# An alignment directive in VectorE's instruction stream, in a log-sum-exp kernel

## Chip, cores and metric

The kernel runs on one core of one Trainium2 chip. The metric is the device time of one execution in microseconds (us), as the median of several. A profiled execution of its own shows where the time goes; its span runs from the first to the last of the program's own instructions.

The engines, as the profile names them: PE is TensorE's matmul and PEld its weight load, DVE is VectorE, ACT is ScalarE, POOL is GpSimd, SP is SyncE. A letter q behind a name means the engine's sequencer: a branch, a semaphore, a register load or the issue of a DMA, during which the engine itself does not compute. Each engine has its own stream of instructions.

## Reference

```python
def reference(x):                       # x: 32 x 512 x 1024, float32
    max_x = np.max(x, axis=-1, keepdims=True)
    return (max_x.squeeze(-1) + np.log(np.sum(np.exp(x - max_x), axis=-1))).astype(np.float32)
```

For each of the 16384 rows of 1024 numbers, one number comes out: the logarithm of the sum of the exponentials.

## The kernel before

The kernel does not subtract the maximum. It computes log(sum(exp(x))) directly, checks that all sums are in a safe range, and only if they are not takes a slow path that does subtract it. The data drawn here are normal, so the slow path is never entered; it stands in the program and is jumped over.

Rows are spread over 128 partitions, 128 rows for each. The input (67 MB) is brought in by 18 loads, all issued by SyncE, whose sizes and treatment the table LOADS lists: three of 16 rows for each partition, then ever smaller ones, the last ones of 0.75 to 1.7 rows. They go into a ring of 48 rows in SBUF. A load waits for those who still use its place in the ring (line 128).

For each load ScalarE takes the exponential in place (line 209). The sum of a row is then made in one of three ways, by the letters of the table: R is a reduction on VectorE (line 220); G lets GpSimd add the right half of each row to the left (line 215), and VectorE reduces the left half later (line 146); T is one VectorE instruction for each row that adds the two halves and accumulates the sum as it goes (line 154, the helper `add_halves`). In the profile each T shows as two rows, a SCALAR_TENSOR_TENSOR and the DVE_READ_ACCUMULATOR behind it. The very last row is split: three quarters of it are summed by ScalarE itself in its exponential (line 204, letter b), the rest by VectorE (letter a).

The order of each engine's instructions is the order in which the Python loop over the loads (line 174) emits them; there is no scheduler. The waits are written by hand: each engine counts a semaphore up with every instruction, and others wait for a count. For the last loads VectorE's stream is: two halves-adding instructions each for the loads with T2, one each for the loads with T1, one for the last (T1+a) and one of 128 columns for the split row. Eight of them come before the sixteenth load (index 15), three after it.

At the end (lines 240 to 264) ScalarE takes the logarithm of the last sums (lines 245 and 247) and SyncE stores them (line 251). At the same time VectorE condenses the sums into a check (lines 161 and 165), TensorE adds the check over the partitions (lines 171, 172 and 255), and VectorE compares the result with a bound (line 259). ScalarE and VectorE both load that flag into a register (line 262) and branch (line 311 in the profile): past the slow path, which has ten instructions on VectorE (lines 288 to 305), or into it. Behind it each of the two counts up the semaphore `done` (lines 311 and 312). SyncE waits for both, clears the semaphores (line 315) and waits for the last store (line 317).

## Time and profile before

| | us |
|---|---|
| median of 3 executions | 162.78 |
| lowest and highest of them | 162.53, 162.91 |
| the profiled execution | 162.55 |
| its span | 161.2 |
| VectorE busy in the span | 119.1 |
| ScalarE busy in the span | 115.1 |
| GpSimd busy in the span | 32.4 |

The input moves at a mean of 417 GB/s over the span. The profiled execution's own time is 1.35 us longer than its span: what lies ahead of the program's first instruction and behind its last. Instructions of a sequencer are not counted as busy; they are found by their source line. In a timeline row the first number is the start and the second the length, both in us.

### The profile page before, as it was taken

Reading aid. Unit: us, or ns where it says so; the run is one execution under the profiler, and the core shown is the slowest. Engines: PE = TensorE matmul, PEld = TensorE weight load, DVE = VectorE, ACT = ScalarE, POOL = GpSimd, SP = SyncE. Lnnn points to the kernel's source line nnn. Section 1 sums busy time; section 2 is a strip of 40 time slices with the busy share of each in tenths; the row PEclk is TensorE's granted clock in tenths of the full one; section 3 lists DMA queues with packets and bytes.
Section 4 is the critical chain, followed back from the end, with each engine's and each line's share of the span. In section 5 each row is a group of like instructions: output and inputs, shape, how many; then the busy total and the mean of one; then the engine's idle time right before and its main releaser. Section 6 shows DMA issues by size and latency. Waiting matters only on the chain.

```text
span 161.2 us, 183 instructions
## 1 busy us (share of the span) xinstructions
PE 0.5 (0%) x10; PEld 0.3 (0%) x10; DVE 119.1 (74%) x48; ACT 115.1 (71%) x32; POOL 32.4 (20%) x15
## 2 busy tenths in 40 slices
PE   0000000000000000000000000000000000000000
PEld 0000000000000000000000000000000000000000
DVE  0000000019999499995999999999999999999995
ACT  3000059980799609994199928996997999799995
POOL 0000000000000000000008800007950806727600
DMA  7996996996996996997999989898998999999990
GB/s 276 504 520 276 504 520 276 504 520 293 488 520 293 488 520 293 488 520 325 429 469 469 469 376 424 377 483 385 454 454 384 419 439 411 409 429 414 424 407 12
DMA packets 2880, 67.18 MB, mean 417 GB/s; under 512 B 576, under 2 KB 576, under 8 KB 1344
## 3 DMA queue, kind: packets, MB, share of 16 engines
q1 hardware_dynamic: 2880, 67.18, 97.2%
HBM read 67.11 MB, written 0.07 MB: 417 GB/s over the span
## 4 chain that ended last, share of the span: by engine, by line
DVE 53%; DMA 30%; ACT 12%; POOL 4%; PE 0%; issue 0%
DVE sumexp L220 38%; DMA ring<-in_x_dram 30%; ACT ring L209 12%; DVE sumexp L146 10%; POOL ring L215 4%; DVE ring L154 4%; DVE clamped L161 1%; DVE total L165 0%; PE count L171 0%; DVE fine L259 0%; PE count L255 0%; PE count L172 0%
## 5 line engine op out<-in xcount | busy, mean ns | idle before, releaser
L209 ACT ACTIVATE ring<-ring 128x16384 f32<-128x16384 f32 (+22 forms) x26 | 112.4, 4371 | 42.7 <-DMA ring<-in_x_dram 42.6
L220 DVE TENSOR_REDUCE sumexp<-ring 128x16 f32<-128x16384 f32 (+6 forms) x10 | 96.1, 9639 | 40.0 <-ACT ring L209 40.0
L215 POOL TENSOR_TENSOR ring<-ring 128x1024 f32<-128x1024 f32 (+5 forms) x9 | 32.1, 3573 | 118.3 <-ACT ring L209 118.3
L146 DVE TENSOR_REDUCE sumexp<-ring 128x2 f32<-128x1024 f32 (+5 forms) x9 | 16.1, 1802 | 0.4 <-POOL ring L215 0.4
L154 DVE SCALAR_TENSOR_TENSOR ring<-ring 128x512 f32<-128x512 f32 (+1 forms) x11 | 6.5, 642 | 0.0
L118 ACT ACT_TABLE_LOAD x1 | 1.3, 1283 | 1.4 <-PEq L59 1.4
L161 DVE SCALAR_TENSOR_TENSOR clamped<-sumexp 128x114 f32<-128x114 f32 (+1 forms) x2 | 0.9, 472 | 0.1
L204 ACT ACTIVATE ring<-ring 128x768 f32<-128x768 f32 x1 | 0.8, 843 | 0.1
L171 PE MATMUL count<-far,bad 128*1 128x1 f32 x4 | 0.4, 163 | 159.1 <-DVE total L165 159.1
L154 DVE DVE_READ_ACCUMULATOR ring<-ring 128x1 f32 x11 | 0.8, 76 | 0.0
L171 PEld LDWEIGHTS count<-far,bad 128*1 128x1 f32 x4 | 0.2, 80 | 159.2 <-POOL ring L215 151.1
L259 DVE TENSOR_SCALAR fine<-count 1x1 int32<-1x1 f32 x1 | 0.1, 146 | 0.4 <-PE count L255 0.4
L165 DVE TENSOR_REDUCE total<-sumexp 128x1 f32<-128x114 f32 (+1 forms) x2 | 0.4, 210 | 0.0
L172 PE MATMUL count<-total,ones 128*1 128x1 f32 x4 | 0.4, 163 | 0.0
L245 ACT ACTIVATE res<-sumexp 128x15 f32<-128x15 f32 x1 | 0.2, 215 | 0.1
L119 POOL MEMSET ones<- 128x1 f32 x1 | 0.1, 98 | 1.0 <-POOLq L59 1.0
L195 ACT ACTIVATE res<-sumexp 128x112 f32<-128x112 f32 x1 | 0.3, 280 | 0.0
L247 ACT ACTIVATE res<-sumexp 128x1 f32<-128x1 f32 x1 | 0.3, 278 | 0.0
L172 PEld LDWEIGHTS count<-total,ones 128*1 128x1 f32 x4 | 0.2, 81 | 0.0
L255 PE MATMUL count<-sumexp,ones 128*1 128x1 f32 x2 | 0.2, 163 | 0.0
L204 ACT ACTIVATION_READ_ACCUMULATOR ring<-ring 128x1 f32 x1 | 0.2, 187 | 0.0
L161 DVE DVE_READ_ACCUMULATOR clamped<-sumexp 128x1 f32 x2 | 0.2, 79 | 0.0
(6 smaller groups left out, 0.6 us busy)
## 6 DMA issues: line engine op xcount, KB each, us to landing
ring<-in_x_dram SPq DMA_DIRECT2D x1, 7376.0 KB, 24.9
ring<-in_x_dram SPq DMA_DIRECT2D x1, 5936.0 KB, 19.6
ring<-in_x_dram SPq DMA_DIRECT2D x1, 4768.0 KB, 16.4
ring<-in_x_dram SPq DMA_DIRECT2D x1, 3520.0 KB, 15.2
ring<-in_x_dram SPq DMA_DIRECT2D x1, 2976.0 KB, 21.9
ring<-in_x_dram SPq DMA_DIRECT2D x1, 1792.0 KB, 27.6
ring<-in_x_dram SPq DMA_DIRECT2D x1, 1520.0 KB, 25.2
ring<-in_x_dram SPq DMA_DIRECT2D x1, 1360.0 KB, 19.5
```

The lines of the kernel that those rows point to most:

```text
L118: nc.scalar.preload_act_table_set("natural_log_exp_and_others")
L146: at = dve.did(nc.vector.reduce_sum(out=sumexp[:, c0 : c0 + s], in_=half, axis=AX.X))
L154: return dve.did(nc.vector.scalar_tensor_tensor(out=lo, in0=lo, scalar=1.0, in1=v[:, h : 2 * h], op0=ALU.mult, op1=ALU.add, accum_out=sume ...
L161: dve.did(nc.vector.scalar_tensor_tensor(out=clamped[:, c0:c1], in0=sumexp[:, c0:c1], scalar=LOW, in1=sumexp[:, c0:c1], op0=ALU.max, op1=A ...
L165: at = dve.did(nc.vector.reduce_sum(out=total[:, k : k + 1], in_=sumexp[:, c0:c1], axis=AX.X))
L171: pe.did(nc.tensor.matmul(count, lhsT=bad[:, k : k + 1], rhs=far, start=k == 0, stop=False))
L172: pe.did(nc.tensor.matmul(count, lhsT=ones, rhs=total[:, k : k + 1], start=False, stop=False))
L195: ln_early = act.did(nc.scalar.activation(out=res[:, 0:W], in_=sumexp[:, 0:W], func=AF.Ln))
L204: last = act.did(nc.scalar.activation(out=v, in_=v, func=AF.Exp, accum_out=sumexp[:, NC : NC + 1]))
L209: at = act.did(nc.scalar.activation(out=v, in_=v, func=AF.Exp))
L215: folded.append((c, p, s, pool.did(nc.gpsimd.tensor_tensor(out=rows[:, :, 0:H], in0=rows[:, :, 0:H], in1=rows[:, :, H:d], op=ALU.add,))))
L220: users.append((p, p + s * d, dve, dve.did(nc.vector.reduce_sum(out=sumexp[:, c : c + s], in_=rows, axis=AX.X))))
```

## The change

A constant names the sixteenth load (index 15), and in the loop, when that load's turn comes, a directive is put into VectorE's stream before its next instruction. It asks the loader to place what follows at a slot whose number is a multiple of 128, and to fill the slots in between with empty instructions. Only VectorE's stream has it. All instructions, waits and loads that were there stay in their order.

```diff
 B = 16
+
+ALIGNED = 15
...
         act.wait(landed[i], 16)
+        if i == ALIGNED:
+            nc.vector.addr_align(128)
         for k, part in enumerate(parts):
```

The next instruction on VectorE after the directive is the halves-adding instruction of that load (line 154, line 156 with the change), the ninth of eleven.

## The prediction

> **What bounds the kernel now.** I read the page first, then the chain of waits in its last microseconds, then VectorE's timeline there, and last the single source lines whose instructions are the sequencers' own and so count as busy nowhere. The page:

> ```profile
> span 161.2 us, 183 instructions
> PE 0.5 (0%) x10; PEld 0.3 (0%) x10; DVE 119.1 (74%) x48; ACT 115.1 (71%) x32; POOL 32.4 (20%) x15
> DVE 53%; DMA 30%; ACT 12%; POOL 4%; PE 0%; issue 0%
> ```

> No engine is full over the whole span; VectorE (DVE) holds more than half of the chain that ends last. The end of that chain, from the view of the chain of waits:

> ```profile
> 155.16 3.89 DVE ring L154 x14
> 159.05 0.02 issue
> 159.07 0.18 DVE clamped L161 x2
> 159.25 0.09 DVE total L165
> 159.34 0.04 issue
> 159.39 0.19 PE count L171 x2
> ...
> 159.71 0.15 DVE fine L259
> ```

> The reader should see two things. From 155.16 to 159.05 any delay of VectorE is a delay of the end. And the chain stops at 159.86 (159.71 + 0.15), while the span ends at 161.2: 1.34 us follow in which no engine is busy. The timeline and the single lines show what stands there:

> ```profile
> 159.50 0.34 SPq L251 DMA_DIRECT2D out_dram<-res  x1
> ...
> L262 ACTq TENSOR_LOAD <-fine x1: 463/463/463, 159.9 to 159.9; - x1
> L262 DVEq TENSOR_LOAD <-fine x1: 544/544/544, 159.9 to 159.9; - x1
> ...
> L311 ACTq COMPARE_BRANCH  x1: 45/45/45, 160.4 to 160.4; - x1
> L311 DVEq COMPARE_BRANCH  x1: 67/67/67, 160.5 to 160.5; - x1
> L311 ACTq EVENT_SEMAPHORE  x1: 17/17/17, 160.5 to 160.5; - x1
> ...
> L312 DVEq EVENT_SEMAPHORE  x1: 21/21/21, 161.0 to 161.0; - x1
> ...
> L315 SPq EVENT_SEMAPHORE_RANGE_CLEAR  x1: 71/71/71, 161.1 to 161.1; - x1
> ...
> L317 SPq EVENT_SEMAPHORE  x1: 17/17/17, 161.2 to 161.2; - x1
> ```

> Durations are in ns, starts in us. ScalarE (ACT) and VectorE both load the flag, branch over the slow path, and count up `done`. ScalarE's branch ends at about 160.4 + 0.045 and its count-up starts at 160.5: 0.1 us between. VectorE's load starts at 159.9 and takes 0.544, so its branch runs at about 160.47 to 160.54; its count-up starts only at 161.0 (160.95 to 161.05). That is 0.41 to 0.51 us for the same jump. SyncE waits for that count-up and then ends the kernel:

> ```profile
> SPq L315 <- DVEq L312: 1.2, 1, 1.2
> ```

> So the tail is set by VectorE's jump, 0.3 to 0.4 us longer than ScalarE's. The other thing the end waits for is the landing of the last store:

> ```profile
> out_dram<-res SPq DMA_DIRECT2D x1, 8.0 KB, 1.4
> ```

> Issued at 159.50, it lands at 160.85 to 160.95 (1.4 as printed), 0.25 to 0.35 before the end: hidden now, but not by much.

> **The change part by part.** One directive goes into VectorE's stream, between the eighth and the ninth of the halves-adding instructions (line 154). No wait, DMA, buffer or arithmetic is added, removed or moved. Two things follow: a filling ahead of the ninth, N slots with N from 0 to 127, and everything behind it lies elsewhere relative to the borders of the blocks in which code is fetched. The place, from VectorE's timeline:

> ```profile
> 154.48 0.67 DVE L146 TENSOR_REDUCE sumexp<-ring 128x1 f32<-128x512 f32 x1
> 155.08 0.67 DVE L154 SCALAR_TENSOR_TENSOR ring<-ring 128x512 f32<-128x512 f32 x1
> ...
> 156.91 0.68 DVE L154 SCALAR_TENSOR_TENSOR ring<-ring 128x512 f32<-128x512 f32 x1
> 157.52 0.07 DVE L154 DVE_READ_ACCUMULATOR ring<-ring 128x1 f32 x1
> 157.52 0.68 DVE L154 SCALAR_TENSOR_TENSOR ring<-ring 128x512 f32<-128x512 f32 x1
> ...
> 158.75 0.28 DVE L154 SCALAR_TENSOR_TENSOR ring<-ring 128x128 f32<-128x128 f32 x1
> 158.96 0.08 DVE L154 DVE_READ_ACCUMULATOR ring<-ring 128x1 f32 x1
> ```

> *Why a jump may be dear.* That code is fetched by DMA in pieces shows in the DMA view of the stretch 161 to 163 us, just after VectorE's jump:

> ```profile
> GB/s 0 0 0 0 0 0 0 0 0 0 0 0 164 0 0 0 0 0 0 0 0 0 0 0 0 0 0 0 0 0 0 0 0 0 0 0 0 0 0 0
> q14 instruction: 1, 0.01, 1.7%
> ```

> One packet of the kind "instruction", at 161.60 to 161.65: 164 GB/s over a slice of 0.05 us is 8.2 KB. The queue table of the page has none inside the span. So somewhere near the end one engine went over the border of a fetched piece and the next was sent for. My reading is that it was VectorE, that its border lies between the branch and its target, and that the extra 0.3 to 0.4 us is the price of going over it.

> [...]

> *The filling.* If the border is there, N can be counted. Behind the directive stand three pairs of line 154, a pair of line 161, lines 165 and 259, the load and the branch: twelve instructions. The slow path has ten more, then the count-up. So the border lies 12 to 22 slots behind the directive, and aligning pulls it forward by that many: N is 12 to 22. The price of an empty slot is not in the trace; the nearest rows:

> ```profile
> L59 DVEq DRAIN  x2: 10/10/10, 0.8 to 1.2; - x2
> L59 DVEq EVENT_SEMAPHORE  x2: 21/21/21, 1.1 to 1.4; - x2
> ...
> 0.23 0.10 POOL L355 MEMSET const-float32-0.0<- 128x1 f32 x1 [0.23 <-issue]
> ...
> 0.34 0.10 POOL L355 MEMSET const-uint8-127<- 128x1 uint8 x1
> ```

> The cheapest sequencer instruction takes 10 ns, the branch above 67; four memsets are issued in 0.11 us, 37 ns apart, though each runs 100. I take 40 ns, near that issue step, with 10 and 67 as bounds. So 12 to 22 slots cost 0.5 to 0.9 us of the sequencer's time, and going over the border there 0.35 more: 0.85 to 1.25 us.

> *What hides it.* VectorE works meanwhile on what its sequencer already queued. If that is one instruction, the sequencer reaches the directive when the eighth addition starts, and the cover is 157.52 - 156.91 = 0.61 us; 0.25 to 0.65 would then show and move the end one for one. If it is the four pairs in front of the directive, the cover is 157.52 - 154.48 = 3.04 us and nothing shows. TensorE's rows say how far a sequencer runs ahead of a blocked instruction:

> ```profile
> 159.38 0.09 PEld L171 LDWEIGHTS count<-far,bad 128*1 128x1 f32 x2 [8.12 <-DVE total L165]
> 159.39 0.19 PE L171 MATMUL count<-far,bad 128*1 128x1 f32 x2 [8.02 <-DVE total L165]
> ...
> 159.49 0.19 PE L255 MATMUL count<-sumexp,ones 128*1 128x1 f32 x2
> ```

> After 8 us of waiting, six loads and six matmuls begin within 0.14 us, some 12 ns apart, far below the issue step: they stood ready. I take the long cover. [...]

> *The gain.* With branch and target in one block the jump should cost VectorE about what ScalarE's does, saving 0.3 to 0.4 us at the count-up. SyncE then clears at about 160.70, is ready by 160.82, and waits for the store that lands at 160.85 to 160.95. Its last instruction follows about 0.03 us later, so the span ends at 160.90 to 161.00: a saving of 0.20 to 0.30. If the store lands a tenth earlier than in the profiled execution, up to 0.40.

> *The fetch.* It moves with the border, to about 155 or 156 us, in among the last loads:

> ```profile
> 152.04:155.08 3.04, 0.00 (x0) 0.00 (x0) 3.04 (x10) 3.04 (x4) 0.00 (x0) 1.00 1.01 418
> 158.01 0.84 ACT L204 ACTIVATE ring<-ring 128x768 f32<-128x768 f32 x1
> 158.76 0.19 ACT L204 ACTIVATION_READ_ACCUMULATOR ring<-ring 128x1 f32 x1
> ```

> 418 GB/s over 16 engines are 26 GB/s each, so 8.2 KB hold one of them for 0.31 us. ScalarE's last exponential is done at 158.95, VectorE at 159.04: 0.09 of cover, so at worst 0.22 is lost, and only where the engine hit is the last to deliver. I count it as nothing and keep 0.22 for the range.

> **Sum.** Filling 0, fetch 0, jump -0.30 (between the two limits of the store): the profiled execution's 162.55 becomes 162.25. The median shown, 162.78, lies 0.23 above that execution, so I forecast 162.48, and 162.35 to 162.65 as this case's own range.

> **The rivals.** (1) *More is saved*: 1.35 us lie behind the span, and the code fetch sits there too. If something there also waited for it, its 8 KB (0.31 us at 26 GB/s) go as well: 162.2. For it speaks only that the packet lies there; no row shows a wait for it.
> (2) *Nothing is saved*: the 0.41 to 0.51 us are VectorE's own price of a taken branch, or the border is elsewhere, and the filling is hidden: 162.8. For it: VectorE jumps only once here, so nothing in this trace separates the two. Against it: VectorE's other sequencer instructions are only 1.2 to 1.5 times as long as ScalarE's (544 to 463, 67 to 45), which turns 0.1 into 0.15, not into 0.46.
> (3) *The filling shows: slower.* It has to be longer than its cover. With 3.04 us of cover and 0.35 for the border this begins at N = 67 ((3.04 - 0.35) / 0.04); at N = 127 it is 5.4 - 3.0 = 2.4 us on VectorE, where every delay in this stretch goes into the end: 165.2, and about 164.0 in the middle between 67 and 127. N above 22 means that the border was not at the jump, so there is no saving against it. With the short cover and N of 12 to 22 the balance is -0.05 to +0.35: up to 163.1. Against it: the count above; for it: it rests on the border being where I put it and on a queue that I see only on TensorE.

> **How the numbers follow.** The forecast 0.60, rival (1) 0.10, (2) 0.09, (3) 0.21. A measurement here can tell about 0.2% or 0.33 us from no change. The forecast's 0.30 is just at that bound, and its size is open by 0.1 to either side, so I split its 0.60 into 0.32 faster and 0.28 same. Faster: 0.32 + 0.10 = 0.42. Same: 0.28 + 0.09 = 0.37. Slower: 0.21. The range goes from 162.1 (rival 1, and the scatter of the runs, which reaches 0.25 below their median) to 163.3 (the short cover with its 163.1, and the collision of the fetch, 0.22 on the forecast or on no gain); what is left out is mostly the longer fillings of rival (3).

> **What would show it.** Right: in the changed kernel VectorE's count-up starts 0.1 to 0.2 us behind its branch instead of 0.41 to 0.51; SyncE's last instruction follows the store's landing; a packet of the kind "instruction" lies inside the span, near 155 to 157 us; and the additions at line 156 still follow each other every 0.61 us without a hole. A hole ahead of the ninth is the filling (or the border) showing, and its length is the loss. A count-up still 0.4 us or more behind the branch makes rival (2) right. A later start of ScalarE's last exponential, against its 158.01, would be the collision of the fetch. The forecast fails altogether if there is a hole longer than 0.3 us.

## The result, and the profile after

| | median, us | runs |
|---|---|---|
| before | 162.65 | 18 |
| with the directive | 162.37 | 18 |

The ratio is 0.9981, with a 95% interval from 0.9975 to 0.9988: the changed kernel is 0.28 us faster. Its profiled execution has a span of 161.0 us against 161.2.

Lines behind the directive now stand four lines further down, those ahead of it two. The single source lines of the changed kernel, which answer to those shown of before (durations in ns, starts in us):

```profile
L186 DVEq NOP  x19: 18/18/18, 156.0 to 156.9; - x19
...
L266 DVEq TENSOR_LOAD <-fine x1: 543/543/543, 159.9 to 159.9; - x1
...
L315 DVEq COMPARE_BRANCH  x1: 72/72/72, 160.5 to 160.5; - x1
...
L316 DVEq EVENT_SEMAPHORE  x1: 21/21/21, 160.7 to 160.7; - x1
...
L319 SPq EVENT_SEMAPHORE_RANGE_CLEAR  x1: 92/92/92, 160.7 to 160.7; - x1
...
L321 SPq EVENT_SEMAPHORE  x1: 17/17/17, 160.9 to 160.9; - x1
```

The filling is visible: 19 empty instructions, within the 12 to 22 that were counted from the place of the branch. They take 0.9 us from the first to the last, and VectorE computes beside them (its addition of 156.30, shown below, runs on to 156.98), so a row with a q is not always a time in which the engine itself does nothing. The register load and the branch stand where they stood (159.9, 160.5), but the count-up of `done` comes at 160.7 and not at 161.0: it follows the end of the branch (160.55 in the trace) by 0.10 to 0.20 us, where it was 0.41 to 0.51. To the nanosecond, which the trace keeps, the two gaps are 0.138 and 0.488 us: the jump has become 0.35 us shorter. SyncE's clearing moves from 161.1 to 160.7 with it.

The last instruction, line 321, is at 160.9. The store that it waits for, from the view of the DMA issues and the timeline of the changed kernel:

```profile
out_dram<-res SPq DMA_DIRECT2D x1, 8.0 KB, 1.4
159.50 0.34 SPq L255 DMA_DIRECT2D out_dram<-res  x1
```

159.50 + 1.4 is 160.9. SyncE is done with its clearing at 160.7 + 0.09, so the store sets the end now. The count-up came 0.3 us earlier; of that the store let a little less through to the end.

The ninth addition, the first instruction behind the filling, in the timeline of the changed kernel:

```profile
156.30 0.68 DVE L156 SCALAR_TENSOR_TENSOR ring<-ring 128x512 f32<-128x512 f32 x1
...
156.91 0.68 DVE L156 SCALAR_TENSOR_TENSOR ring<-ring 128x512 f32<-128x512 f32 x1
157.53 0.08 DVE L156 DVE_READ_ACCUMULATOR ring<-ring 128x1 f32 x1
157.53 0.68 DVE L156 SCALAR_TENSOR_TENSOR ring<-ring 128x512 f32<-128x512 f32 x1
```

It starts at 157.53 against 157.52, with no hole ahead of it. And the code packet has moved; the DMA view of the changed kernel from 157 to 159 us, in slices of 0.05 us:

```profile
GB/s 397 336 177 178 180 197 153 72 45 0 0 0 0 0 0 0 0 0 0 0 164 0 0 0 0 0 0 0 0 0 0 0 0 0 0 0 0 0 0 0
...
q14 instruction: 1, 0.01, 1.1%
```

The 164 GB/s in the slice from 158.00 are the same 8.2 KB that were sent for at 161.60 before. The loads' packets are down to nothing by 157.45 in this view. Only VectorE's stream was changed and the packet moved with it, so I take it that it was VectorE that went over a border near the end. In these two runs the packet follows the border by some 1.1 us: 158.0 against the last empty slot at 156.9 here, 161.60 against the branch's end at 160.54 before.

### The profile page after: what moved, and what is told of

Its sections match the earlier page's. It is cut to its first block, busy times and chain, and to the rows that moved or that the text cites. A ratio compares the mean times of both kernels' runs of the same rounds, so it can differ in the third digit from the quotient of the medians.

```text
span 161.0 us, 202 instructions
## 1 busy us (share of the span) xinstructions
PE 0.5 (0%) x10; PEld 0.3 (0%) x10; DVE 119.1 (74%) x48; ACT 115.0 (71%) x32; POOL 32.4 (20%) x15
## 4 chain that ended last, share of the span: by engine, by line
DVE 52%; DMA 30%; ACT 12%; POOL 4%; issue 1%; DVEq 0%; PE 0%
DVE sumexp L224 38%; DMA ring<-in_x_dram 30%; ACT ring L213 12%; DVE sumexp L148 10%; POOL ring L219 4%; DVE ring L156 3%; DVE clamped L163 1%; DVEq L186 0%; DVE total L167 0%; PE count L173 0%; DVE fine L263 0%; PE count L259 0%; PE count L174 0%
## 5 line engine op out<-in xcount | busy, mean ns | idle before, releaser
L251 ACT ACTIVATE res<-sumexp 128x1 f32<-128x1 f32 x1 | 0.3, 279 | 0.0
L259 PE MATMUL count<-sumexp,ones 128*1 128x1 f32 x2 | 0.2, 163 | 0.0
```

## The experiments

Each was timed in turn with the kernel before, on the same chip. Only the place and length of the filling differ, except in the last pair. Ratios are to the kernel before.

**Where the border lies: 9, 8 and 7 filled slots.** The alignment takes an offset; what follows then starts that many slots into a block. With 118, 117 and 116 the filling is 9, 8 and 7 slots, and the border falls ahead of the load, between load and branch, and between branch and target.

```diff
-            nc.vector.addr_align(128)
+            nc.vector.addr_align(128, offset=118)   # 117, 116
```

> Same place for the directive, but only 9 filled slots instead of 19, so the border falls ahead of VectorE's register load (line 266), behind the comparison (line 263). My theory: going over a border costs VectorE's sequencer about 0.35 us wherever it stands, and shows only where the sequencer has not run ahead. Here it runs ahead while the comparison still waits for TensorE, so nothing shows: load at 159.9, count-up 0.14 us behind the branch, time as the changed kernel (0.998 of before). Rival A, only a jump into another block costs: the same numbers here. Rival B, the gain comes from the ninth addition starting a block: no gain, 1.000 of before, gap 0.45 us.

> 8 filled slots: the border falls between the register load and the branch, so it is crossed in a straight line, by a sequencer that has nothing to run ahead of. My theory (any crossing costs 0.35 us): the branch starts 0.35 to 0.40 us behind the end of the load instead of 0.03, the count-up 0.14 behind the branch, time as before (1.000, 162.65). Rival A (only a taken branch into another block costs): branch 0.03 behind the load, time as the changed kernel (0.998).

> 7 filled slots: the branch is the last slot of its block, its target 11 slots into the next one. Both theories: the count-up comes 0.41 to 0.51 us behind the branch as in the kernel before, time 1.000 of before. If the length of the jump into the new block mattered, the gap would differ from that of before, where by the count of 19 the border was 8 slots behind the branch.

Single lines of the run with 9 slots:

```profile
L266 DVEq TENSOR_LOAD <-fine x1: 535/535/535, 160.0 to 160.0; - x1
...
L315 DVEq COMPARE_BRANCH  x1: 72/72/72, 160.5 to 160.5; - x1
...
L316 DVEq EVENT_SEMAPHORE  x1: 21/21/21, 160.7 to 160.7; - x1
```

With 8 slots:

```profile
L266 DVEq TENSOR_LOAD <-fine x1: 534/534/534, 159.9 to 159.9; - x1
...
L315 DVEq COMPARE_BRANCH  x1: 72/72/72, 160.9 to 160.9; - x1
...
L316 DVEq EVENT_SEMAPHORE  x1: 21/21/21, 161.1 to 161.1; - x1
```

With 7 slots:

```profile
L315 DVEq COMPARE_BRANCH  x1: 67/67/67, 160.5 to 160.5; - x1
...
L316 DVEq EVENT_SEMAPHORE  x1: 21/21/21, 161.1 to 161.1; - x1
```

One slot decides. With 9 the load follows the comparison at once, the branch the load, the count-up the branch: 162.41 us, 0.9989 (0.9980 to 0.9998). With 8 the load ends at about 160.5 (159.9 + 0.53) and the branch starts only at 160.9, 0.4 us late, while the count-up follows the branch closely: 162.69 us, 1.0006 (0.9997 to 1.0015). With 7 the gap is behind the branch again: 162.60 us, 1.0001 (0.9992 to 1.0010). So rival A falls: a border costs about as much in a straight line (0.41 us) as in the jump (0.35, and 0.31 with 7 slots). Rival B falls too, since with 9 slots the ninth addition begins no block and the gain is there.

With 9 slots the code packet tells when the code behind the border was there. The DMA view of this run from 157 to 159 us, and the comparison, which is the last instruction ahead of the border, in its timeline:

```profile
GB/s 388 292 292 162 214 152 135 90 36 27 0 0 0 0 0 0 0 0 0 164 0 0 0 0 0 0 0 0 0 0 0 0 0 0 0 0 0 0 0 0
...
q14 instruction: 1, 0.01, 1.2%
...
159.77 0.15 DVE L263 TENSOR_SCALAR fine<-count 1x1 int32<-1x1 f32 x1 [0.38 <-PE count L259]
```

The packet is there at 157.95, 1.8 us before the comparison starts. At that time the comparison still waits for TensorE, and the check ahead of it for VectorE's own last addition, which ends at 159.09. So the code behind the border, which lies ten slots behind the last empty one, was sent for well ahead of the end of these waits, and the border cost nothing here: the load follows the comparison at once (160.0 against 159.77 + 0.15), and the time is 162.41 us. With 8 slots the register load, which has a wait of its own, stands ahead of the border, and the packet came only at 161.60, 1.1 us behind the end of that load.

**What a crossing and a slot cost: 40 slots.**

```diff
-            nc.vector.addr_align(128)
+            nc.vector.addr_align(128, offset=21)
```

> The directive at the sixteenth load again, but with 40 filled slots: the border is met after 19 of them and 21 more follow. If a crossing costs VectorE's sequencer 0.41 us (as in the run with 8) and a slot 0.047, the filling takes 40 x 0.047 + 0.41 = 2.3 us against 1.52 us of cover (the first slot began 1.52 us ahead of the ninth addition), so a hole of about 0.8 us opens ahead of the ninth addition, in the filled slots there is one step of 0.46 us after the 19th, and the time is 1.003 to 1.004 of before (+0.8 for the hole, -0.27 for the jump). If the sequencer can run ahead further than seen (3.0 us), no hole and 0.998. If a crossing between empty slots is free, a hole of 0.35 us and 1.0005.

The chain of waits of this run goes through the empty slots (start, length in us); around the 19th it reads

```profile
157.08 0.03 issue
157.11 0.02 DVEq L186
157.13 0.46 DVE ring L156 x2
157.59 0.03 issue
157.62 0.02 DVEq L186
157.64 0.03 issue
157.67 0.02 DVEq L186
```

A slot takes 0.02 and the way to the next 0.03: 0.047 us, as the 40 slots show that stand between 156.2 and 158.5 with the one long step. That step, between the 19th and the 20th, lasts 157.59 - 157.13 = 0.46 (the chain fills it with the addition that ran meanwhile), 0.41 more than an ordinary one. This is the border by itself. The timeline shows what came of it:

```profile
158.57 0.69 DVE L156 SCALAR_TENSOR_TENSOR ring<-ring 128x512 f32<-128x512 f32 x1 [0.77 <-ACT ring L213]
```

A hole of 0.77 us. The releaser named there is not the cause, since ScalarE's exponential had long ended; the empty slots are. Time 163.22, 1.0039 (1.0025 to 1.0053), as expected from the crossing at full price.

**How large a block is: alignment to 256.**

```diff
-            nc.vector.addr_align(128)
+            nc.vector.addr_align(256)
```

> Alignment to 256 slots in place of 128. If the blocks in which code is fetched have 256 slots, the border of before is a multiple of 256, the filling is 19 again and the time that of the changed kernel (0.998). If they have 128 and the border of before is an odd multiple, the filling is 147 slots with two borders in it: 147 x 0.047 + 2 x 0.41 = 7.7 us less 1.52 of cover, a hole of 6.2 us, two steps of 0.46 us in the filled slots, two packets of code, time 168.5 (1.036). If it is an even multiple nothing can be told of the size.

The line of the filling, the queue table, and the ninth addition in the timeline of this run:

```profile
L186 DVEq NOP  x147: 18/18/18, 156.3 to 163.6; - x147
...
q14 instruction: 2, 0.02, 0.0%
...
164.00 0.69 DVE L156 SCALAR_TENSOR_TENSOR ring<-ring 128x512 f32<-128x512 f32 x1 [6.40 <-issue]
```

**The directive at the first load.**

```diff
-ALIGNED = 15
+ALIGNED = 0
```

> The directive at the first load, ahead of all of VectorE's work, where VectorE waits some 35 us for its first input. From the places in the stream I count 55 filled slots, 2.6 us at 47 ns, all hidden. My theory: branch and target are in one block as in the changed kernel, gap 0.14 us, 0.998 of before. Rival B (the place of the border within the additions matters): 1.000. A time below the changed kernel's would mean that the filling at the sixteenth load, or the fetch of code there, still cost something.

The run did worse than before: 162.99 us, 1.0025 (1.0015 to 1.0035). The filling was 57 slots (two more than counted) and lay well ahead of any work. The jump was cured: branch at 161.2, count-up at 161.4. What was lost is at the other end. First the changed kernel's timeline, ScalarE's first exponential:

```profile
21.80 13.86 ACT L213 ACTIVATE ring<-ring 128x16384 f32<-128x16384 f32 x1 [19.07 <-DMA ring<-in_x_dram]
```

The same row with the directive at the first load, the filling, and the code packet in the DMA view from 9.0 to 9.5 us:

```profile
22.50 13.86 ACT L213 ACTIVATE ring<-ring 128x16384 f32<-128x16384 f32 x1 [19.77 <-DMA ring<-in_x_dram]
...
L186 DVEq NOP  x57: 18/18/18, 1.5 to 4.1; - x57
...
q14 instruction: 1, 0.01, 3.9%
```

The border was met at about 4.1 us, the code came only at 9 us, in between the packets of the loads, and the first load was taken up 0.70 us later. From there on everything is later by that much: at the end of the chain of waits the comparison (line 263) starts at 160.42, and at 159.72 in the changed kernel.

The same place without a border: with 9 filled slots the border lies where it lay in the run with 9 at the sixteenth load.

```diff
-ALIGNED = 15
+ALIGNED = 0
...
-            nc.vector.addr_align(128)
+            nc.vector.addr_align(128, offset=80)
```

> The directive at the first load again, but with 9 filled slots (offset 80), so that no border is met there: it falls behind the comparison (line 263) as in the run with 9 slots. No code is fetched among the loads. My theory (the 0.6 us lost with the directive at the first load are the 8 KB of code among the loads): first load lands with no late engine, the code is fetched near 158 us, jump gap 0.14, time as the changed kernel, 0.998. If filled slots at the start, or a directive there, cost anything by themselves: still above 1.000.

```profile
21.82 13.86 ACT L213 ACTIVATE ring<-ring 128x16384 f32<-128x16384 f32 x1 [19.08 <-DMA ring<-in_x_dram]
```

In its timeline the first exponential starts at 21.82, as in the changed kernel. The time is 162.48, 0.9995 (0.9986 to 1.0004): 0.5 us better than with the border there, so the packet among the loads was the loss. That this run reaches the changed kernel's time is not shown; its interval includes 1. In its profile one more thing differs: the check of 114 columns took 1.00 us, against 0.75 in the changed kernel (more on it in the last section).

**The directive at the seventh and at the eleventh load.**

```diff
-ALIGNED = 15
+ALIGNED = 6     # and 10
```

> The directive at the seventh load (index 6), ahead of a 1.7 us reduction near 128 us, with VectorE's reductions of 2 to 5 us ahead of it as cover. Jump gap 0.14 as in the changed kernel. The run at the first load was 0.6 us slower because the code fetched there (8 KB) went in among the loads and the first load landed 0.6 us late; at 128 us VectorE has no idle time and loads are ahead of it, so the same delay of one load should be hidden: 0.998. If the fetch among loads always costs, wherever they are ahead or not: 1.0025.

> The directive at the eleventh load (index 10), near 151 us: the border is passed there with the filling hidden (about 36 slots and a crossing, 2.1 us, behind reductions), and the code is fetched at about 151 to 154 us among the last loads, which ScalarE takes up as they land. Jump gap 0.14. If the delay of 0.6 us seen at the first load hits one of the last loads: ScalarE's exponentials behind it up to 0.6 late, VectorE's last additions late by up to 0.5 (0.1 of cover), time up to 1.0015. If it hits a load that is not waited for: 0.998.

Both missed. At the seventh load: 163.19 us, 1.0031 (1.0019 to 1.0044). The filling, the code packet in the DMA view from 128 to 129 us, and ScalarE and VectorE in the timeline:

```profile
L186 DVEq NOP  x47: 18/18/18, 121.8 to 124.0; - x47
...
q14 instruction: 1, 0.01, 2.1%
...
131.92 6.16 ACT L213 ACTIVATE ring<-ring 128x3776 f32<-128x3776 f32 x2 [0.89 <-DMA ring<-in_x_dram]
...
149.37 1.22 DVE L148 TENSOR_REDUCE sumexp<-ring 128x2 f32<-128x1024 f32 x1 [0.25 <-POOL ring L219]
150.62 1.17 DVE L163 SCALAR_TENSOR_TENSOR clamped<-sumexp 128x114 f32<-128x114 f32 x1
```

ScalarE waits 0.89 us for a load at 131, where the changed kernel has no wait. I had expected that VectorE, which had work in hand, would swallow it. It did until 149 us: there VectorE waits for GpSimd, which waited for the late ScalarE, and the check behind it takes 1.17 us where it took 0.77 in the kernel before. The delay did not shrink on the way: the exponential of 1856 columns, which waits for a load in both, starts at 139.00 here and at 138.01 in the changed kernel. It was paid for at the first place without slack.

At the eleventh load it is 163.72 us, 1.0068 (1.0054 to 1.0081), and the loss is the filling itself:

```profile
L186 DVEq NOP  x37: 18/18/18, 150.3 to 152.1; - x37
...
149.08 1.21 DVE L148 TENSOR_REDUCE sumexp<-ring 128x2 f32<-128x1024 f32 x1
150.33 0.77 DVE L163 SCALAR_TENSOR_TENSOR clamped<-sumexp 128x114 f32<-128x114 f32 x1
...
152.53 1.22 DVE L148 TENSOR_REDUCE sumexp<-ring 128x2 f32<-128x1024 f32 x1 [1.24 <-POOL ring L219]
```

The first empty slot came at 150.3, when line 163 had started, and not long before. Line 163 waits for VectorE's own reduction (`dve.wait(dve, dve.n)`), which ends at 149.08 + 1.21 = 150.29, and the empty slots behind it had not begun before that. So 37 slots and a crossing, 2.15 us, stood against 0.9 us of work: a hole of 1.24.

**What holds the empty slots: one load earlier.**

```diff
-ALIGNED = 15
+ALIGNED = 14
```

> The directive one load earlier (index 14), ahead of the eighth addition: 21 filled slots. In the runs so far the first filled slot came 0.04 us after the last count that an instruction ahead of it waits for (155.970 to 156.011 in the changed kernel). Theory W: a wait that is not met yet holds VectorE's sequencer, met ones do not. Ahead of the eighth addition that is the exponential of load 13, which ends at 154.78: first slot near 154.82. Theory Q: the sequencer is held by a queue of five instructions, and the first slot comes 1.52 us ahead of the eighth addition (156.91): near 155.4. Either way 21 x 0.047 + 0.41 = 1.4 us fit, no hole, jump gap 0.14, 0.998 of before; the code is fetched about 1.1 us behind the border, near 157.3 (W) or 157.9 (Q), and by W it can meet the last loads, for up to 0.2 us.

The filling and ScalarE's exponential for load 13 in this run, with its length from the groups by form:

```profile
L186 DVEq NOP  x21: 18/18/18, 154.9 to 155.8; - x21
...
153.20 2.82 ACT L213 ACTIVATE ring<-ring 128x1728 f32<-128x1728 f32 x2
...
L213 ACT ACTIVATE ring<-ring 128x1728 f32<-128x1728 f32 x1 | 1.6, 1627 | 0.0
```

That exponential ends at 153.20 + 1.63 = 154.83, and the first empty slot is at 154.9; theory Q, with the 1.52 us of the changed kernel ahead of 156.91, would have put it near 155.4. The changed kernel fits as well, with the exponential of load 14:

```profile
154.68 2.96 ACT L213 ACTIVATE ring<-ring 128x1312 f32<-128x1312 f32 x3
...
L213 ACT ACTIVATE ring<-ring 128x1312 f32<-128x1312 f32 x1 | 1.3, 1281 | 0.0
```

154.68 + 1.28 = 155.96, first empty slot at 156.0. So for the empty slots theory W holds in both and in the run at the eleventh load. It does not hold for the fetch of code: with 9 slots the packet came at 157.95, while instructions ahead of the border still waited, up to the comparison at 159.77. Time 162.35, 0.9986 (0.9977 to 0.9995).

**What bounds the end now: an earlier last logarithm.** In line 245 (249 with the change) the logarithm of 15 columns waits for all additions, though it needs them only up to the tenth.

```diff
     sums = dve.n
-    act.wait(dve, sums)
+    act.wait(dve, max(at for c0, _, at in summed if c0 < LAST))
...
     act.wait(act, last)
+    act.wait(dve, sums)
```

It was run with the directive and without.

> The changed kernel, and in it ScalarE's logarithm of the 15 last columns but one waits only for VectorE's tenth addition, no longer for the eleventh, so it runs beside that one and the very last logarithm, and with it the last store, comes 0.10 to 0.12 us earlier. My theory: in the changed kernel the store's landing sets the end (last instruction of SyncE 0.016 us behind it); here it lands near 160.80, and SyncE is ready at 160.87, so the end moves by 0.05 to 0.08 us and is set by VectorE's count-up: span 160.87 to 160.90, 0.9975 to 0.998 of before. If the end hangs on something else: unchanged against the changed kernel, or the full 0.12.

> The same earlier logarithm without the directive: the store lands 0.12 us earlier, but VectorE's jump with its border still sets the end: 1.000 of before, jump gap 0.41 to 0.51.

```profile
159.37 0.08 DVE L156 DVE_READ_ACCUMULATOR ring<-ring 128x1 f32 x1
...
159.87 0.34 SPq L256 DMA_DIRECT2D out_dram<-res  x1
...
L48 ACTq EVENT_SEMAPHORE  x1: 17/17/17, 159.5 to 159.5; - x1
```

With the directive the store is issued 159.87 - 159.45 = 0.42 us behind the end of the last addition, where the changed kernel needs 159.50 - 159.04 = 0.46: 0.04 won and not 0.12. The second wait became an instruction of its own on ScalarE, 17 ns at 159.5. (All rows of this profiled execution stand some 0.4 us late, the ninth addition at 157.93 against 157.53; only the differences count.) 162.48 us, 0.9987 (0.9978 to 0.9996): no better than the changed kernel. Without the directive it is 162.78, 1.0009 (1.0000 to 1.0018): nothing won, as expected while the jump sets the end. No version tried beat the change beyond the intervals.

## Why the prediction was right

*The border between branch and target.* Right, and now shown from three sides: the filling is 19, inside the counted 12 to 22; the code packet moved with the border; and shifting the border by single slots moves the lost time from behind the branch to ahead of it and then out of sight. The sum took 0.35 us for a crossing; in the jump it measured 0.35, between empty slots 0.41.

*The gain.* The forecast of 162.48 was made against a median of 162.78, a saving of 0.30; measured were 0.28, against 162.65. The limit by the store's landing, 0.20 to 0.30 in the profiled execution, is what the profile after shows. The time of 162.37 lies at the lower edge of the forecast's own range, 162.35 to 162.65, because the median of before came out 0.13 lower with more runs; the saving itself was right to 0.02. Rival (1), more saved behind the span, did not come: what the profiled execution takes outside its span is 1.3 us in both kernels (162.29 less 161.0, 162.55 less 161.2). Rival (2), nothing saved, is refuted by the count-up at 160.7 with the branch and its distance to the target unchanged.

*The filling.* The price per slot was 40 ns in the sum and is 47; with 19 slots and a crossing that makes 0.9 + 0.4 = 1.3 us, just above the predicted 0.85 to 1.25.

*The cover.* This is the term that was mis-sized. I took 3.04 us, four pairs of additions ahead, as an estimate from how TensorE's instructions started together after a long wait; no run shows the 3.04 or the four pairs on VectorE. What the runs showed in its place is that the empty slots began when the last count awaited ahead of them arrived: at 156.0 in the changed kernel (exponential done at 155.96), at 154.9 one load earlier (154.83), at 150.3 at the eleventh load (150.29). The cover here is therefore what VectorE still had to do at that moment: from 156.0 to 157.53, 1.5 us, between the 0.61 and the 3.04 that the prediction weighed. Against 1.3 of filling and crossing that leaves 0.2. The forecast held with a margin of 0.2 us, not 1.8, and that it was enough is luck: by these prices four or five slots more would have begun to show. Rival (3), the filling that shows, starts not at 67 slots but, as an estimate, at about 23 ((1.5 - 0.41) / 0.047), and the runs with 40 and 147 are it.

*The fetch.* I put it at 155 to 156 us, in among the last loads, and counted it as nothing, with 0.22 as the worst. It came at 158.0, with the loads all in, because the empty slots began later than I thought and the packet came 1.1 us behind the border. That it costs nothing here is right: the last addition starts at 158.75, as before. As a price for code that meets loads, 0.31 us of one DMA engine (0.22 of them lost) was too low: 0.70 at the first load.

## What to carry to other kernels

Look for time between an engine's branch and its target that no busy row covers, and compare it with another engine that does the same jump. If a fetch border lies there, moving it to a place with cover saves at most what the crossing costs, 0.35 us here, once, and no more than the next wait behind it allows (0.28 here). Measure the cover from the last awaited count ahead of the directive (1.5 us here), set against it the price of each filled slot and of the border (0.047 and 0.41 us in the run with 40 slots), and keep the fetch away from loads that set the pace (0.70 us lost at the first load).

## What the runs showed of the hardware that I had not expected

A crossing cost VectorE's sequencer 0.41 us in a straight line (8 and 40 slots) and 0.31 to 0.35 in the jump (7 slots, and the kernel before). It did not show in the time where VectorE still had work in hand (no hole at 157.53 in the changed kernel), nor with 9 slots, where the code was there before the waits ahead of the border were over.

In three runs the empty slots did not pass an instruction whose wait was not met; once the waits were met they started at once, within the rounding of 0.1 us of the rows shown (156.0 against 155.96, 154.9 against 154.83, 150.3 against 150.29). The code behind a border came past such instructions all the same: with 9 slots the packet was there at 157.95, 1.8 us before the comparison ahead of the border. What makes the difference was not shown.

One packet of code of 8.2 KB among the loads made the first load be taken up 0.70 us later, and ScalarE wait 0.89 us for a later one. The traces show where. A load counts its semaphore up in sixteen parts here, and a single part was late: at the first load fifteen had landed by 21.89 us and the last only at 22.48, where all had by 21.78 in the changed kernel. With the directive at the seventh load the load that ScalarE waits for had fifteen parts by 131.11 and the last at 131.90, and every load behind it in that trace, too, has one part some 0.8 us behind the others. At 26 GB/s on one DMA engine, the sixteenth part of the 418 GB/s measured before, those bytes are 0.31 us, as an estimate; why it becomes twice that and more stays open. The packet itself came 1.1 us behind the border where no load was left, and 4 to 5 us behind it in the midst of the loads (9 against 4.1, 128.4 against 124.0).

In the run with the directive at the seventh load the check of 114 columns took 1.17 us on VectorE against 0.77 in the kernel before. In both it ends 0.14 us behind the end of the GpSimd addition that runs beside it (151.65 and 151.79 in this run, 150.66 and 150.80 in the kernel before), and so it does in the changed kernel, with 0.75 us (150.66 and 150.80). So in these runs its length follows how late GpSimd is; whether GpSimd's addition holds it, no run tests.
